# A token-mixing trunk on one core: one head's softmax weights turned by transfers, stores on another queue, turning loads at later steps, last rows in smaller pieces

## The chip, the cores and the metric

The kernel runs on one core of one Trainium2 chip. A core has a matrix engine (TensorE, PE in the profile, with its weight loads as PEld), a vector engine (VectorE, DVE), an activation engine (ScalarE, ACT), GpSimd (POOL), a queue engine (SyncE, SP) and 16 DMA engines that all queues share. SP, ScalarE and GpSimd can issue transfers. The metric is the device time of one execution in microseconds; lower is better.

## The reference

Two layers over 256 latent tokens and 256 context tokens of width 1024, in float32. Layer 0 mixes tokens with a two-way chunked mLSTM of 4 heads, layer 1 with latent attention of 8 heads; each is followed by a gated convolutional FFN, with adaptive modulation and a LayerNorm after every part. The output is the 256 latent rows. The part of the mLSTM that the change touches is, for one head:

```python
dmat = jnp.where(tril, b[..., :, None] - b[..., None, :] + ic[..., None, :], -jnp.inf)
wmat = jnp.exp(dmat - mj[..., None]) * jnp.einsum("bhjd,bhsd->bhjs", qc, kc)
num = g[..., None] * jnp.einsum("bhjd,bhde->bhje", qc, C) + jnp.einsum("bhjs,bhse->bhje", wmat, vc)
h = num / jnp.maximum(jnp.abs(den), jnp.exp(-mj))[..., None]
...
hsum = o * s.transpose(0, 2, 1, 3).astype(h_in.dtype)
return _head_rms_norm(hsum, norm_g) @ w_out
```

and at the very end `(z - mean) * rsqrt(var) * g + b` on the output rows.

## The kernel before

Every float32 product is done as three products of a high and a low part (`mm3`, lines 447, 450, 451): high by high, high by low, low by high. Weights stream from memory through `Stream`: SP loads a block of 128 x 1024 (`raw`), ScalarE casts its high part (line 361), VectorE subtracts the low part (line 384). Three buffers (`NB`) hold split weights, and a buffer is filled again when TensorE is through with it.

The mLSTM is computed without its chunks: for each head `h`, `w_qk(h, ...)` makes queries and keys (four products of 16 blocks, eight weights of 24 matmuls), `s_mm(h)` the scores, `head(h, ...)` the weights of the four row blocks `P[0..3]` (each a tile `W` with an offset), and `av(h)` multiplies them by the values. Row blocks 0 and 1 are context tokens and see only context columns, blocks 2 and 3 see all four column blocks. `av` needs the weights turned, columns on partitions: `head` turns twelve 128 x 128 blocks in three groups of four on TensorE (line 1144) into a PSUM tile `PT`, which `split` cuts into high (ScalarE, line 461) and low part (VectorE, line 462).

`head` is a generator that runs beside the products of the next head. `tick` takes one step of such background work, two steps after each of the eight weights in `w_qk`; `drain` runs what is left. So head 0's weights are made and turned during `w_qk(1)`, and `av(0)` follows it. `post(h, ...)` normalises a head's rows. For heads 0 and 1 it cuts each float32 row into two planes of 16 bits (`planes`, ScalarE, line 466), stores them to DRAM (line 1225, from GpSimd's queue), and `turn_load` (line 1266) loads them transposed from ScalarE's queue; `turn_split` (lines 1274, 1275) scales and cuts them for the output projection. `mixed` interleaves this with the next head's `head` steps by a plan written as a string: each word is a step, `p` a step of `post`, `h` one of `head`, `L` a load, `S` a split.

The program order is a wish: a planner orders each engine's instructions by priority and by its own estimate of when operands are ready, unless an order is pinned. Tiles tagged `s2` (128 x 512 floats, 15 of them) and `u` (31 pairs) are shared by all this work. `ln_rows` with `fin` is the end of the kernel: it normalises two blocks of 128 output rows in halves of 512 columns (lines 1314, 1316; the first half of the first block on ScalarE and GpSimd, lines 1318 to 1320) and stores each half (line 1321), the first half from SP, the second from ScalarE.

Of the kernel before, what the change touches and what calls it, by code (L numbers as in the profile page):

```python
# [10 lines left out]
U16 = mybir.dt.uint16  # L11
AF = mybir.ActivationFunctionType
ALU = mybir.AluOpType
# [21 lines left out]
NB, NRAW, NU, NS = 3, 3, 31, 15  # L35
# [381 lines left out]
class K:  # L417
# [648 lines left out]
    def head(self, h, S, big=False):  # L1066
        nc, last = self.nc, big
        aB = [self.s2("aB0"), self.s2("aB1")]
        for d in range(2):
            nc.gpsimd.dma_start(aB[d], self.ad[d, h:h + 1, :].to_broadcast([128, 512]))  # L1070
        if not big:
            self.t4_step(2)
        Am = [self.s2("Am0"), self.s2("Am1")]
        for d in range(2):
            nc.vector.tensor_tensor(Am[d].rearrange("p (t s) -> p t s", t=4),
                                    aB[d].rearrange("p (t s) -> p t s", t=4),
                                    self.mask[:, d:d + 1, :].to_broadcast([128, 4, 128]), op=ALU.add)
        yield
        full = {0: [(0, 0), (0, 128), (0, 256), (0, 384)], 1: [(128, 256), (0, 0), (0, 256), (0, 256)]}
        P = []  # L1080
        for g in range(3):
            jbs = [0, 1] if g == 0 else [g + 1]
            if big:
                w = self.uf("W")
                W = [w[:, 0:512], w[:, 512:1024]]
            else:
                W = [self.s2("W0"), self.s2("W1")]
            den = self.tiny(4, "den")
            nd = len(jbs)
            rng = {}  # L1090
            for i, t in enumerate(jbs):
                base = 256 * i if g == 0 else 0
                for d in range(2):
                    o = W[d]
                    bias = self.gcol[:, 0, t, 32 * d + h:32 * d + h + 1]
                    spans = [(t * 128, (t + 1) * 128, Am[d])]
                    if d == 0:
                        if t > 0:
                            spans.append((0, t * 128, aB[d]))
                        lo, hi = 0, (t + 1) * 128  # L1100
                    else:
                        if t == 0:
                            spans.append((128, 256, aB[d]))
                        if t >= 2:
                            spans.append((0, 256, aB[d]))
                        if t == 2:
                            spans.append((384, 512, aB[d]))
                        lo, hi = {0: (0, 256), 1: (128, 256), 2: (0, 512), 3: (0, 512)}[t]
                    if d == 1 and t == 3:
                        nc.vector.memset(o[:, 256:384], 0.0)  # L1110
                    for s0, s1, src in spans:
                        nc.scalar.activation(o[:, base + s0:base + s1], src[:, s0:s1], AF.Exp, bias=bias, scale=1.0)
                    nc.vector.scalar_tensor_tensor(o[:, base + lo:base + hi], o[:, base + lo:base + hi], 1.0,
                                                   S[g][:, base + lo:base + hi], op0=ALU.mult, op1=ALU.mult,
                                                   accum_out=den[:, 2 * i + d:2 * i + d + 1])
                    rng[i, d] = (base + lo, base + hi)
            dv = den[:, 0:2 * nd]
            R = self.tiny(4, "R")
            nc.vector.scalar_tensor_tensor(R[:, 0:2 * nd], dv, -1.0, dv, op0=ALU.mult, op1=ALU.max)
            e = self.gcol[:, 1, jbs[0]:jbs[-1] + 1, h::32]  # L1120
            nc.vector.tensor_tensor(R[:, 0:2 * nd].rearrange("p (t d) -> p t d", d=2),
                                    R[:, 0:2 * nd].rearrange("p (t d) -> p t d", d=2), e, op=ALU.max)
            nc.vector.reciprocal(R[:, 0:2 * nd], R[:, 0:2 * nd])
            for i, t in enumerate(jbs):
                big = {0: 1, 1: 0, 2: 1, 3: 0}[t]
                b0, b1 = rng[i, big]
                s0, s1 = rng[i, 1 - big]
                nc.vector.tensor_scalar(W[big][:, b0:b1], W[big][:, b0:b1], R[:, 2 * i + big:2 * i + big + 1], None,
                                        op0=ALU.mult)
                nc.vector.scalar_tensor_tensor(W[big][:, s0:s1], W[1 - big][:, s0:s1],  # L1130
                                               R[:, 2 * i + 1 - big:2 * i + 2 - big], W[big][:, s0:s1],
                                               op0=ALU.mult, op1=ALU.add)
                P.append((W[big], b0))
            yield
        for _ in range(5 if last else 1):
            yield
        self.PT = []
        for grp in ([(t, s) for s in range(2) for t in (0, 1)], [(t, s) for s in range(2) for t in (2, 3)],
                    [(t, s) for s in (2, 3) for t in (2, 3)]):
            pt = self.ps("PT")  # L1140
            lead = None
            for n, (t, s) in sorted(enumerate(grp), key=lambda x: -x[1][0] * (x[1][0] > 1)):
                src, b0 = P[t]
                q = nc.tensor.transpose(pt[:, n * 128:(n + 1) * 128], src[:, b0 + s * 128:b0 + (s + 1) * 128], self.ident)
                if lead is None:
                    lead = q
                elif t > 1:
                    self.behind(q, [lead])
            u = self.u("PT")
            self.split(u[:, 0], u[:, 1], pt)  # L1150
            self.PT.append(u)
        yield

    def v_load(self, h):
# [34 lines left out]
    def av(self, h):  # L1189
        nc = self.nc  # L1190
        PT, v = self.PT, self.vh
        ts = []
        for t in range(4):
            ps = self.ps("av")
            if t < 2:
                blocks = [(PT[0], s, s) for s in range(2)]
            else:
                blocks = [(PT[1], s, s) for s in range(2)] + [(PT[2], s, s + 2) for s in range(2)]
            for n, (u, i, s) in enumerate(blocks):
                c = slice(i * 256 + (t % 2) * 128, i * 256 + (t % 2) * 128 + 128)  # L1200
                self.mm3(ps, (u[:, 0, c], u[:, 1, c]), (v[s][:, 0], v[s][:, 1]), n == 0, n == len(blocks) - 1)
            ts.append(ps)
        for t in range(4):
            nc.vector.tensor_tensor(self.oh[t], ts[t], self.oh[t], op=ALU.mult)
        r = self.oh
        self.PT = self.vh = self.oh = None
        return r

    def post(self, h, tt, last=False):
        nc = self.nc  # L1210
# [9 lines left out]
        if not last:  # L1220
            d = self.dr.tile([512, 2, 512], U16, name="hd")
            for t in range(4):
                pl = self.pool.tile([128, 2, 512], U16, tag="s2", name="pl", bufs=NS)
                self.planes(pl, tt[t])
                nc.gpsimd.dma_start(d[t * 128:(t + 1) * 128], pl)
            self.turned.append((h, d, 0))
            yield
            return
# [15 lines left out]

    def mixed(self, head, post):

        plan = "p hp h hL h hL . L hS LS h S S . . ."
        for step in plan.split():
            for op in step:
                if op in "hp":  # L1250
                    next(head if op == "h" else post, None)
                elif op == "L":
                    self.turn_load()
                elif op == "S":
                    self.turn_split()
            yield
# [29 lines left out]
    def ln_rows(self, pss, xres, gate, fin=None):  # L1286
# [3 lines left out]
        for t in range(2):  # L1290
# [16 lines left out]
            fine = len(pss[1]) > 2  # L1307
            if fin is not None:
                g, b, out = fin
                for c0, c1 in ((0, 512), (512, 1024)):  # L1310
                    c, h = slice(c0, c1), c0 // 512
                    hc = slice(c0 - h * 512, c1 - h * 512)
                    if t or c0 == 512:
                        nc.vector.scalar_tensor_tensor(z[:, c], z[:, c], mv[:, 0:1], g[h][:, hc],
                                                       op0=ALU.subtract, op1=ALU.mult)
                        nc.vector.scalar_tensor_tensor(z[:, c], z[:, c], rs, b[h][:, hc], op0=ALU.mult, op1=ALU.add)
                    else:
                        nc.scalar.activation(z[:, c], z[:, c], AF.Identity, bias=nm, scale=rs)
                        nc.gpsimd.tensor_tensor(z[:, c], z[:, c], g[h][:, hc], op=ALU.mult)
                        nc.gpsimd.tensor_tensor(z[:, c], z[:, c], b[h][:, hc], op=ALU.add)  # L1320
# [1241 lines left out]
```

## Time and profile before

| | |
|---|---|
| median of 3 runs | 1338.72 us (1338.04 to 1338.85) |
| the profiled execution | 1337.94 us |
| its span, first to last instruction | 1336.1 us |
| TensorE busy | 1325.5 us, 99% |
| VectorE, ScalarE, GpSimd busy | 1075.4, 729.0, 165.4 us |
| mean DMA rate | 244 GB/s |
| TensorE in the granted clock | 0.998 |

The span is counted between the first and the last instruction; the execution's own time has 1.84 us around it. In rows of the timeline the columns are start, length, engine, line, operation, output and inputs; in brackets is how long the engine had idled before and whose end released it. Times within the profile are counted from the span's start. ACTq and SPq are the issues of transfers on the queues of these engines.

### The profile page before, as it was taken

What the parts mean: (1) busy time and instruction counts of PE and PEld (TensorE: products, weight loads), DVE (VectorE), ACT (ScalarE), POOL (GpSimd) and SP (SyncE); (2) the same over time, 40 slices, a digit from 0 to 9 for tenths busy, and PEclk for the clock granted to TensorE, in tenths of its full rate; (3) what the DMA queues carried; (4) which work ended last, traced back from release to release, by engine and by line L of the source; (5) the groups of instructions that cost most, each with busy time, mean ns of one, the idle gap of its engine ahead of it and who ended that gap; (6) DMA issues with size and microseconds to landing.
All of it is one profiled execution on the core that took longest, in us unless ns stands there. A gap on an engine that the chain in (4) does not pass through costs nothing.

```text
span 1336.1 us, 18732 instructions
## 1 busy us (share of the span) xinstructions
PE 1325.5 (99%) x6573; PEld 1111.9 (83%) x6573; DVE 1075.4 (80%) x1783; ACT 729.0 (55%) x1271; POOL 165.4 (12%) x268
## 2 busy tenths in 40 slices
PE   9999999999999999999999999999999999999997
PEld 5777888888888888888898888888888988988886
DVE  4798957678688596987879977758899889899995
ACT  4765544445734555574744333333567768577771
POOL 0212000011110111120002011112000022110010
PEclk9999999999999999999999999999999999999999
DMA  9988948789675487876628989967976597499790
GB/s 364 331 276 288 338 160 257 238 270 313 236 262 189 155 248 199 297 275 212 222 79 275 324 259 284 281 174 177 329 232 211 180 244 206 151 309 310 227 334 33
DMA packets 116991, 325.52 MB, mean 244 GB/s; under 512 B 21417, under 2 KB 40361, under 8 KB 116625
## 3 DMA queue, kind: packets, MB, share of 16 engines
q1 hardware_dynamic: 64288, 223.37, 48.9%
q0 software_dynamic: 33360, 81.43, 22.7%
q10 hardware_dynamic: 19248, 19.54, 4.5%
q8 instruction: 51, 0.84, 0.2%
q14 instruction: 44, 0.35, 0.1%
HBM read 289.51 MB, written 56.80 MB: 259 GB/s over the span
## 4 chain that ended last, share of the span: by engine, by line
PE 99%; DMA 0%; DVE 0%; SPq 0%; issue 0%; DVEq 0%; ACT 0%
PE fin L1570 8%; PE y L450 6%; PE y L447 6%; PE y L451 6%; PE tok L447 6%; PE tok L450 6%; PE tok L451 6%; PE fin L450 6%; PE fin L447 6%; PE fin L451 6%; PE qk L447 4%; PE qk L451 4%; PE qk L450 4%; PE up L743 2%; PE up L447 2%; PE up L450 1%
## 5 line engine op out<-in xcount | busy, mean ns | idle before, releaser
L361 ACT CAST w<-raw 128x1024 fp32r<-128x1024 f32 (+2 forms) x280 | 289.8, 1037 | 257.4 <-PE tok L451 73.3
L384 DVE TENSOR_TENSOR w<-raw,w 128x1024 fp32r<-128x1024 f32 (+2 forms) x280 | 335.2, 1200 | 114.7 <-ACT w L361 110.7
L566 DVE SCALAR_TENSOR_TENSOR junk<-ar,bc 128x1024 f32<-128x1024 f32 x128 | 155.7, 1216 | 4.9 <-ACT bc L608 2.6
L450 PE MATMUL fin<-h,w 128*128 128x512 f32 (+1 forms) x370 | 139.6, 377 | 0.0
L447 PE MATMUL fin<-h,w 128*128 128x512 f32 (+1 forms) x370 | 139.5, 377 | 0.0
L451 PE MATMUL fin<-h,w 128*128 128x512 f32 (+1 forms) x370 | 139.3, 377 | 0.0
L1570 PE MATMUL fin<-h,w 128*128 128x512 f32 (+1 forms) x636 | 113.0, 337 | 0.0
L1570 PEld LDWEIGHTS fin<-h,w 128*128 128x128 f32 x636 | 98.4, 189 | 13.4
L447 PE MATMUL qk<-xc,w 128*128 128x512 f32 x256 | 100.1, 391 | 0.0
L451 PE MATMUL qk<-xc,w 128*128 128x512 f32 x256 | 99.7, 389 | 0.0
L450 PE MATMUL qk<-xc,w 128*128 128x512 f32 x256 | 99.6, 389 | 0.0
L447 PEld LDWEIGHTS fin<-h,w 128*128 128x128 f32 x370 | 69.6, 188 | 12.9
L451 PEld LDWEIGHTS fin<-h,w 128*128 128x128 f32 x370 | 69.6, 188 | 12.8
L450 PEld LDWEIGHTS fin<-h,w 128*128 128x128 f32 x370 | 69.6, 188 | 12.7
L384 DVE TENSOR_TENSOR wu<-raw,wu 128x1024 fp32r<-128x1024 f32 (+1 forms) x52 | 61.9, 1206 | 2.8 <-ACT wu L361 2.5
L451 PEld LDWEIGHTS qk<-xc,w 128*128 128x128 f32 x256 | 48.1, 188 | 10.1
L450 PEld LDWEIGHTS qk<-xc,w 128*128 128x128 f32 x256 | 48.1, 188 | 9.9
L447 PEld LDWEIGHTS qk<-xc,w 128*128 128x128 f32 x256 | 48.1, 188 | 9.8
L361 ACT CAST wu<-raw 128x1024 fp32r<-128x1024 f32 (+1 forms) x52 | 52.9, 1046 | 4.9 <-DMA raw<-in_ws 4.9
L760 ACT ACTIVATE fg<-fg 128x512 f32<-128x512 f32 (+1 forms) x44 | 23.1, 525 | 56.3 <-DVE fg L758 50.2
L447 PE MATMUL tok<-w,hT 128*128 128x512 f32 x128 | 49.9, 390 | 0.0
L450 PE MATMUL tok<-w,hT 128*128 128x512 f32 x128 | 49.8, 389 | 0.0
(520 smaller groups left out, 3153.7 us busy)
## 6 DMA issues: line engine op xcount, KB each, us to landing
raw<-in_ws SPq DMA_DIRECT2D x279, 512.0 KB, 5.0
ar<-in_adaT SPq DMA_DIRECT2D x80, 512.0 KB, 5.7
t4d<-in_ws POOLq DMA_DIRECT2D x20, 512.0 KB, 8.2
zd<-in_ws POOLq DMA_DIRECT2D x18, 512.0 KB, 9.9
adaw<-in_ada SPq DMA_DIRECT2D x16, 512.0 KB, 7.9
raw<-zd SPq DMA_DIRECT2D x12, 512.0 KB, 6.1
zr<-fd ACTq DMA_DIRECT2D x33, 128.0 KB, 5.3
xmd<-xr POOLq DMA_DIRECT2D x16, 256.0 KB, 4.7
```

The costliest lines, as they stand in the source:

```text
L361: self.cast = k.nc.scalar.copy(h[:, :cols], src)
L384: i = self.k.nc.vector.tensor_sub(l[:, :n], src, h[:, :n])
L447: q = mm(out, w[0], x[0], start=start, stop=False, skip_group_check=on)
L450: mm(out, w[0], x[1], start=False, stop=False, skip_group_check=on)
L451: mm(out, w[1], x[0], start=False, stop=stop, skip_group_check=on)
L566: nc.vector.scalar_tensor_tensor(o, w, 1.0, self.bc[j], op0=ALU.mult, op1=ALU.mult, accum_out=col[:, k, j:j + 1])
L743: nc.tensor.matmul(ps[m], wk[i][:, c], hT[k][:, j], start=made[m] == 0, stop=made[m] == 23)
L760: nc.scalar.activation(tmp[:, :n], tmp[:, :n], AF.Silu)
L1570: self.nc.tensor.matmul(ps[:, 0:256] if x else ps, w[x][:, k * 128:(k + 1) * 128], h[:, 0:256] if x else h, start=i == 0 and not k0, stop= ...
```

## The change

Head 0's weights are no longer turned on TensorE. `head` hands over to a new generator `head_turn`, which cuts the weights of each row block into 16-bit planes on ScalarE, stores them with six transfers to three DRAM tiles, loads them with six transposing transfers, all from ScalarE's queue, into three `wx` tiles, and splits these into the same high and low parts as before. Its steps fill the sixteen that `w_qk(1)` offers. Heads 1 to 3 turn on TensorE as before. The turned pieces are now kept in a dictionary by (row block, column block), and `av` reads it in the same order.

The plane stores of `post` are issued from ScalarE's queue and not from GpSimd's. The plan of `mixed` has its loads and splits at later steps. In `ln_rows` the second half of the second block of output rows is scaled and stored as two pieces of 256 columns, the first from ScalarE's queue, the second from SP's; the subtraction before it is still one instruction of 512.

```diff
+        if h == 0:
+            yield from self.head_turn(P)
+            return
         for _ in range(5 if last else 1):
             yield
...
+    def head_turn(self, P):
+        nc = self.nc
+        ds = [self.dr.tile([256, 2, 256], U16, name="w%d" % i) for i in range(3)]
+        for g, wait in enumerate((1, 3, 1)):
+            for _ in range(wait):
+                yield
+            pl = self.pool.tile([128, 2, 512], U16, tag="s2", name="pl", bufs=NS)
+            for t, c in ((0, slice(0, 256)), (1, slice(256, 512))) if g == 0 else ((g + 1, slice(0, 512)),):
+                self.planes(pl[:, :, c], P[t][0][:, c])
+            for i in range(2):
+                c = slice(i * 256, (i + 1) * 256)
+                t = i if g == 0 else g - 1
+                nc.scalar.dma_start(ds[1 + i if g else 0][t * 128:(t + 1) * 128], pl[:, :, c])
+        xs = [self.s2("wx") for _ in range(3)]
+        self.PT = {}
+
+        def load(i, j):
+            nc.scalar.dma_start_transpose(xs[i][:, j * 256:(j + 1) * 256].bitcast(U16),
+                                          ds[i].rearrange("t h n -> (t h) n")[:, j * 128:(j + 1) * 128])
+
+        def cut(i):
+            u = self.u("PT")
+            self.split(u[:, 0], u[:, 1], xs[i])
+            for j in range(2):
+                for t in range(2):
+                    self.PT[t + 2 * (i > 0), j + 2 * (i > 1)] = u, slice(j * 256 + t * 128, j * 256 + t * 128 + 128)
+
+        for ls, c in ([(0, 0)], ()), ([(0, 1)], ()), ([(1, 0), (1, 1)], ()), ([(2, 0), (2, 1)], (0,)), ((), (1,)), ((), (2,)):
+            yield
+            for x in ls:
+                load(*x)
+            for x in c:
+                cut(x)
         yield
...
-                nc.gpsimd.dma_start(d[t * 128:(t + 1) * 128], pl)
+                nc.scalar.dma_start(d[t * 128:(t + 1) * 128], pl)
...
-        plan = "p hp h hL h hL . L hS LS h S S . . ."
+        plan = "p hp h h h h . L hL hL L S S S S ."
...
-                for c0, c1 in ((0, 512), (512, 1024)):
+                for c0, c1 in ((0, 512), (512, 768), (768, 1024)) if t else ((0, 512), (512, 1024)):
                     c, h = slice(c0, c1), c0 // 512
                     hc = slice(c0 - h * 512, c1 - h * 512)
                     if t or c0 == 512:
-                        nc.vector.scalar_tensor_tensor(z[:, c], z[:, c], mv[:, 0:1], g[h][:, hc],
-                                                       op0=ALU.subtract, op1=ALU.mult)
+                        if c0 < 768:
+                            x = slice(c0, h * 512 + 512)
+                            nc.vector.scalar_tensor_tensor(z[:, x], z[:, x], mv[:, 0:1], g[h],
+                                                           op0=ALU.subtract, op1=ALU.mult)
                         nc.vector.scalar_tensor_tensor(z[:, c], z[:, c], rs, b[h][:, hc], op0=ALU.mult, op1=ALU.add)
```

More of the change, by code (lines that the diff above doesn't have):

```diff
@@ L1134, in head @@
             yield
+        if h == 0:
+            yield from self.head_turn(P)
+            return
         for _ in range(5 if last else 1):
             yield
-        self.PT = []
+        self.PT = {}
         for grp in ([(t, s) for s in range(2) for t in (0, 1)], [(t, s) for s in range(2) for t in (2, 3)],
@@ L1150, in head @@
             self.split(u[:, 0], u[:, 1], pt)
-            self.PT.append(u)
+            for n, x in enumerate(grp):
+                self.PT[x] = u, slice(n * 128, (n + 1) * 128)
+        yield
[13 more added lines that the diff above has]
+        xs = [self.s2("wx") for _ in range(3)]
+        self.PT = {}
+        def load(i, j):
[8 more added lines that the diff above has]
+        for ls, c in ([(0, 0)], ()), ([(0, 1)], ()), ([(1, 0), (1, 1)], ()), ([(2, 0), (2, 1)], (0,)), ((), (1,)), ((), (2,)):
+            yield
+            for x in ls:
+                load(*x)
+            for x in c:
+                cut(x)
         yield
@@ L1194, in av @@
             ps = self.ps("av")
[L1195 to L1201, printed above, removed]
+            n = 2 if t < 2 else 4
+            for s in range(n):
+                u, c = PT[t, s]
+                self.mm3(ps, (u[:, 0, c], u[:, 1, c]), (v[s][:, 0], v[s][:, 1]), s == 0, s == n - 1)
             ts.append(ps)
```

## The prediction

> **What bounds the kernel now.** I read the page's busy times and its chain first, then the waits of TensorE, then the chain in order of time, then the stages and groups around the edited places.
>
> ```profile
> PE 1325.5 (99%) x6573; PEld 1111.9 (83%) x6573; DVE 1075.4 (80%) x1783; ACT 729.0 (55%) x1271; POOL 165.4 (12%) x268
> PE 99%; DMA 0%; DVE 0%; SPq 0%; issue 0%; DVEq 0%; ACT 0%
> PE idle L680 <- DVE adav L519: 1.5, 1, 1.5
> PE adar L531 <- DMA adaw<-in_ada: 0.3, 1, 0.3
> PE up L743 <- DVE hT L718: 0.3, 1, 0.3
> ```
>
> The last three lines are all the waits TensorE has in the whole span, 2.1 us, and all belong to the start. From there to its last matmul TensorE never waits, and the chain that ended last is 99% TensorE. So two things alone can move the time: the number and pitch of TensorE instructions, and the few microseconds after the last matmul. Work taken off ScalarE, GpSimd or a queue is worth nothing by itself; work put on them costs nothing until it makes TensorE wait. The granted clock is 1.00 in every window row below, so no clock gain is to be had.
>
> **Part 1: head 0's turn leaves TensorE.** The pieces of the chain with the turning instruction of line 1144 (start, length, count), and its group:
>
> ```profile
> 417.25 0.44 PE PT L1144 x4
> 419.76 0.87 PE PT L1144 x8
> 485.36 1.31 PE PT L1144 x12
> L1144 PE MATMUL PT<-ident,W x48: 270/272/275, 417.1 to 590.9; 128*128 128x128 f32 x48
> 400.76:445.60 44.84, 44.84 (x205) 37.25 (x204) 37.03 (x81) 19.49 (x43) 2.68 (x5) 1.00 0.54 173
> ```
>
> 48 instructions in four heads, 12 to a head, each 272 ns long in its row; but they overlap in the pipeline, and on the chain head 0's twelve take 0.44 + 0.87 = 1.31 us, the same as the next head's twelve (1.31). The last line is the stage of head 1's query/key products (window, length, TensorE busy, loads, VectorE, ScalarE, GpSimd, clock, DMA share, GB/s): 44.84 us of 44.84 busy. Without 1.31 it is 43.53 us for its 192 matmuls, 0.227 each. I take 1.31 us off.
>
> What replaces it lies on ScalarE, VectorE and the DMAs. The nearest rows are those of the products that an existing part already turns by transfers (columns min/median/max in ns):
>
> ```profile
> L466 ACT COPY pl<-oh x8: 1038/1046/1054, 458.7 to 519.7; 128x1024 uint16<-128x1024 uint16 x8
> L1266 ACTq DMA_TRANSPOSE hx<-hd x8: 1177/1215/1401, 470.8 to 533.5; - x8
> DMA to landing us min/median/max: 3.2/3.6/4.5
> L848 ACTq DMA_DIRECT2D od<-o x16: 326/327/423, 135.7 to 201.1; - x16
> L1225 POOL DMA_DIRECT2D hd<-pl x8: 539/543/547, 460.0 to 521.1; - x8
> 429.53 1.05 ACT L361 CAST w<-raw 128x1024 fp32r<-128x1024 f32 x1 [3.59 <-PE qk L451]
> 430.62 1.23 DVE L384 TENSOR_TENSOR w<-raw,w 128x1024 fp32r<-128x1024 f32 x1 [1.25 <-ACT w L361]
> ```
>
> ScalarE gets plane copies of 3 x 1024 elements (3 x 1.05 = 3.1 us), six stores (6 x 0.33 = 2.0) and six turning loads (6 x 1.2 = 7.3 if the half-size ones cost as much, 3.6 if they scale). At most 12.4 us, on an engine with 44.84 - 19.49 = 25 us free in that stage. The three casts and three subtractions of the turned weights stay, reading another memory. A load waits on ScalarE's queue for its stores to land, and behind it stand the casts of the next weights (L361), for which TensorE waits. How much it can be held: three weight buffers, each used for 24 x 0.227 = 5.44 us, so a buffer released is needed again 10.9 us later; cast and subtraction were done at 430.62 + 1.23 = 431.85, 2.3 us after the cast's start; 8.6 us are left. A store landing in 3 to 5 us does not use them up. If it did, each further microsecond would be one of TensorE. Cost taken: 0; bounds 0 to the rival's price below. No gain is possible here, as TensorE has no wait to lose.
>
> When the pieces are there: first group of turns starts at 417.09 = 400.76 + 3 x 5.44, exactly after the third weight, where the background's sixth step stands in the code, so TensorE follows the written order. In the new text the last four loads stand after the seventh weight (400.76 + 7 x 5.44 = 438.85). Were they issued only there, the last of them would go at 438.85 + 3 x 1.2 = 442.5, land 3.6 later at 446.1, and be cast and subtracted (0.62 + 0.68) by 447.4.
>
> ```profile
> 445.65 0.39 PE L447 MATMUL av<-v,PT 128*128 128x512 f32 x1
> 418.22 0.75 DVE L1130 SCALAR_TENSOR_TENSOR W<-W,R 128x512 f32<-128x512 f32 x1
> L461 ACT CAST v<-vr x4: 619/622/622, 435.5 to 437.0; 128x512 fp32r<-128x512 f32 x4
> L462 DVE TENSOR_TENSOR v<-vr,v x4: 684/684/685, 436.2 to 438.0; 128x512 fp32r<-128x512 f32 x4
> 457.99 0.39 PE L447 MATMUL qk<-xc,w 128*128 128x512 f32 x1
> 475.79 1.26 ACTq L1266 DMA_TRANSPOSE hx<-hd  x1
> ```
>
> The product with the values would start at 445.65 - 1.31 = 444.3, and it reaches the third piece after 18 matmuls, at 444.3 + 4.1 = 448.4: 1.0 us spare in the latest order. In the earliest order (weights of the last row block ready at 418.97, copy, store and load after it, some 10 us) the pieces are there by 430. The planner issues such loads ahead of their place in the text: head 2's products start at 457.99, the fourth turning load stands there after the fifth weight (457.99 + 27.2 = 485.2), and it went at 475.79. So I take the early case: no wait.
>
> **Part 2: plane stores from GpSimd's queue to ScalarE's, later turning loads.** Eight stores leave GpSimd (8 x 0.54 = 4.3 us) for ScalarE (8 x 0.33 = 2.6 us, two stages). On GpSimd they stood waiting for the copies, with the broadcasts of the next head's gates behind them:
>
> ```profile
> POOL hd L1225 <- ACT pl L466: 82.3, 6, 49.2
> DVE Am L1075 <- DMA aB<-ad: 15.1, 4, 5.9
> 470.71 0.40 ACT L1112 ACTIVATE W<-Am,gcol 128x128 f32<-128x128 f32 x1 [4.09 <-DVE Am L1075]
> 445.00:491.00 46.00, 46.00 (x216) 38.47 (x215) 31.55 (x70) 28.23 (x57) 8.54 (x16) 1.00 0.75 224
> 475.00:480.00 5.00, 5.00 (x24) 4.14 (x23) 4.93 (x16) 3.15 (x10) 2.96 (x6) 1.00 1.05 173
> 485.00:490.00 5.00, 5.00 (x30) 4.27 (x29) 4.87 (x8) 3.95 (x7) 0.54 (x1) 1.00 1.04 401
> raw<-in_ws SPq DMA_DIRECT2D x1, 512.0 KB, 8.3
> raw<-in_ws SPq DMA_DIRECT2D x279, 512.0 KB, 5.0
> 486.05 1.05 ACT L361 CAST w<-raw 128x1024 fp32r<-128x1024 f32 x1 [4.24 <-DMA raw<-in_ws]
> ```
>
> Those broadcasts can go earlier, and ScalarE's 4.09 us at 470.71 shrink. TensorE is busy 46.00 of 46.00 us in that stage regardless, so this is worth 0 between the bounds: no gain, and no loss while ScalarE has 18 us idle. The turning loads are hard on the DMAs: all engines taken at 173 GB/s where plain transfers reach 401 at the same share, and one weight load beside them landed after 8.3 us against 5.0; a cast waited 4.24 us for it, and even so TensorE did not. Loads placed later meet the value loads instead; the cover is again the three buffers. The splits of the turned rows move a few steps later inside the same stage, and their first reader is the output projection after the next stages. Cost 0.
>
> The Trainium skill, "Advanced Engine Details and Errata", section X-Bar Transpose (TRN2), holds transposing DMAs to be as fast as regular ones, about 90% of a copy. The two 5 us windows (173 against 401 GB/s) disagree, and the measurement decides. By the page, contention in either stage would be no rival; the sum is the same by both.
>
> **Part 3: last rows in smaller transfers.** What follows the last matmul:
>
> ```profile
> 1328.16 0.42 DVE L1297 SCALAR_TENSOR_TENSOR z<-xres,z 128x256 f32<-128x256 f32 x1
> 1330.89 0.66 DVE z L1316
> 1330.81 1.41 DVE L1316 SCALAR_TENSOR_TENSOR z<-z,rs,br 128x512 f32<-128x512 f32 x2
> 1332.25 0.34 ACTq L1321 DMA_DIRECT2D out_dram<-z  x1
> DMA to landing us min/median/max: 2.1/2.1/2.1
> GB/s 0 0 0 0 0 0 0 82 377 385 205 0 0 0 0 0 0 0 0 0 0 82 393 360 377 393 369 99 33 25 0 0 0 0 0 0 0 0 0 0
> ```
>
> The second half of the second row block is now scaled and shifted as two pieces of 256 columns instead of one of 512. One of 512 takes 0.66 us in the chain, one of 256 between 0.33 and 0.44 (the dependent 0.42 plus its gap): the last piece is ready 0 to 0.22 us later; I take 0.08. Its transfer is half as large: the present one lands 2.1 us after issue, and its 0.26 MB at some 380 GB/s are 0.69 us, so half saves 0 to 0.34. But the first half's transfer still starts at the same time and the rate row (0.23 us a slice) shows the engines full from there on, so little of it comes through; I take 0.18. Together -0.1, bounds -0.34 to +0.22.
>
> **Sum.** -1.31 - 0.1 = -1.41 us. The profiled execution took 1337.94 us (span 1336.1 and 1.84 around it), so it would be 1336.5; the median of the runs shown is 1338.72, 0.78 above the profiled one, and on it the forecast is 1337.3 us, -0.11%. About 0.2% (2.7 us) is what a measurement of this kernel can tell from no change, so this counts as within it.
>
> **The rivals.**
> *Late turned weights (slower).* The last turning load meets other transfers on full DMA engines and takes as long as such transfers took beside the other turning loads:
>
> ```profile
> oh<-od POOLq DMA_DIRECT2D x2, 256.0 KB, 10.3
> ```
>
> 10.3 instead of 3.6 in the latest order makes the third piece late by 6.7 - 1.0 = 5.7 us; TensorE waits in the product with the values: 1337.3 + 5.7 = 1343.0 us. It is slower by over 0.2% from 4.1 us of wait on, a landing 8.7 us after issue in that order. For it: the 8.3 and 10.3 us rows. Against it: this stage has a DMA share of 0.54, and the early order has 15 us more. Chance 0.12.
>
> *A small wait somewhere (no measurable change).* All engines' orders after the edit are planned anew, and a wait of 1 to 4 us where there is none now, in this stage or a later one, eats the gain or turns it: 1338.3 to 1341.3, 1339.8 in the middle. For it: margins like the 1.0 us above, and the cast that waited 4.24. Against it: 2.1 us of waits in the whole span. Chance 0.22.
>
> *Each turn is worth its whole row (faster).* If the twelve cost their 272 ns and not their chain share, 12 x 0.272 = 3.3 us go: 1338.72 - 3.3 - 0.1 = 1335.3, -0.25%. Against it: the stage's 44.84 us hold 192 matmuls of 0.227 and leave 1.31. Chance 0.06.
>
> *Fewer small transfers win at the end.* If the last transfer's landing does not shrink with its size and the extra instruction costs its 0.22, part 3 is +0.22: 1337.6. The Trainium skill, "SBUF — State Buffer", section The DMA setup-cost knee, speaks for it: about 2 us a transfer whatever its size, so coalesce. Its fit gives an estimate of 2.6 us for 256 KB and 2.3 for 128 KB; the row has 2.1 for 256 KB, below both. It changes the hundredths only and lies inside the main case.
>
> **How the numbers follow.** Main case 0.60 at 1337.3, its own range 1336.7 to 1338.0; the small wait 0.22, late weights 0.12, the whole row 0.06. Within 0.2%: 0.60 + 0.22 = 0.82; slower 0.12; faster 0.06. The range takes the main case, nearly all of the small wait and the lower half way to 1335.3: 1336.2 to 1340.8.
>
> **What will show it.** Twelve instructions of line 1144 fewer, and TensorE idle still only in the start's waits: right. The stage of head 1's products at 43.5 us: right. A wait of the value product on the turned weights, or of any matmul on a weight's subtraction: wrong, by its length. The last output transfer issued near 1331.0 (1332.25 - 1.31 + 0.08) and the span ending 3.7 us after it (now 3.85) would confirm the tail. A cast held over 8 us behind a turning load would refute the cover I named.

## The result: slower, and the profile after

| | before | after |
|---|---|---|
| median, measured together | 1338.38 us (1337.82 to 1338.85, 4 runs) | 1357.07 us (1351.47 to 1360.96, 4 runs) |
| the profiled execution | 1337.94 us | 1358.53 us |
| its span | 1336.1 us | 1356.6 us |

The ratio is 1.0135, 95% interval 1.0115 to 1.0154. The forecast was 1337.3 us, its upper bound 1340.8. The four executions after the change lie 9.5 us apart; what follows is read from one of them.

The page's busy times and clock digits of the changed kernel (40 slices of 33.9 us), then every wait of TensorE (total us, times, longest):

```profile
PE 1330.7 (98%) x6561; PEld 1115.2 (82%) x6561; DVE 1074.9 (79%) x1784; ACT 731.6 (54%) x1275; POOL 161.2 (12%) x260
PEclk9999999999999979999999999999999999999999
PE PT L1147 <- DVE W L1130: 15.8, 3, 10.8
PE idle L680 <- DVE adav L519: 1.5, 1, 1.5
PE up L743 <- DVE hT L718: 0.3, 1, 0.3
```

Twelve instructions fewer on TensorE, as the change says, yet 5.2 us more busy time, and a wait that did not exist: TensorE's turn of the weights of heads 1 to 3 (`PT`, now line 1147) waits for VectorE's last scaling of `W` in all three heads, 10.8, 0.9 and 4.1 us. The longest begins near 484.65, in the middle of head 2's query and key products, where head 1's weights are turned. What ScalarE, VectorE and GpSimd did there (start, length; in brackets the idle time before and what ended it; ACTq is the issue of a transfer on ScalarE's queue):

```profile
468.27 1.26 ACTq L1304 DMA_TRANSPOSE hx<-hd  x1
473.37 1.18 ACTq L1304 DMA_TRANSPOSE hx<-hd  x1
474.58 7.19 ACTq L1304 DMA_TRANSPOSE hx<-hd  x1
481.86 11.34 ACTq L1304 DMA_TRANSPOSE hx<-hd  x1
493.24 0.19 ACT L581 COPY adav<-w 1x1 f32<-1x1 f32 x1 [11.14 <-issue]
493.34 0.57 ACT L461 CAST qk<-qk 128x512 fp32r<-128x512 f32 x1
493.94 0.69 DVE L462 TENSOR_TENSOR qk<-qk 128x512 fp32r<-128x512 f32 x1 [10.27 <-ACT qk L461]
494.55 0.74 DVE L1130 SCALAR_TENSOR_TENSOR W<-W,R 128x512 f32<-128x512 f32 x1
495.44 1.94 PE L1147 MATMUL PT<-ident,W 128*128 128x128 f32 x8 [10.79 <-DVE W L1130]
471.86 2.18 POOL L1200 DMA_DIRECT2D vr<-vd  x4 [26.11 <-DVE W L1113]
474.14 0.63 POOL L1206 DMA_DIRECT2D oh<-od  x1
```

Read it upwards from TensorE's row. The turn waited for the scaling of `W`, which took only 0.74 us, but stood on VectorE behind the subtraction of `qk`; that waited 10.27 us for ScalarE's cast; and the cast stood on ScalarE's queue behind the *issues* of the third and fourth turning loads, which held the engine for 7.19 and 11.34 us. The product that it casts was done by about 479 (the products start at 456.85, and its four weights take 4 x 5.44 us); in the kernel before, the same cast ran at 479.95. Before the change an issue took at most 1.40 us. Nothing in the data orders the scaling of `W` behind a turning load: two in-order queues did.

What the long issues have beside them is seen in the neighbours: GpSimd's loads of the values and gates (`vr`, `oh`) start at 471.86, and three of the four turning loads after them. In the kernel before, the four went at 470.83 to 475.79, the first value load at 475.70. The turning loads' group and landing before, the same after, and the DMA queues in a window of before (470.5 to 475) and two of after (480 to 490, 490 to 500), as packets, MB and share of the 16 engines; q10 holds the turning loads, q0 GpSimd's:

```profile
L1304 ACTq DMA_TRANSPOSE hx<-hd x8: 1176/2504/11335, 468.3 to 549.5; - x8
DMA to landing us min/median/max: 18.8/19.3/20.9
...
q10 hardware_dynamic: 2010, 0.51, 68.8%
...
q10 hardware_dynamic: 1260, 0.31, 61.2%
q0 software_dynamic: 212, 0.68, 48.0%
...
q10 hardware_dynamic: 1646, 0.41, 68.9%
```

(The 3.2/3.6/4.5 us landing of before stands in the prediction.) Before, turning loads moved 0.51 MB in 4.5 us, some 113 GB/s, with a quarter of the engines' time going to SP's plain loads. After, they moved 0.31 MB in 10 us beside the value and gate loads and 0.41 MB in the next 10 us, in which SP's plain loads (34.8%) had mostly taken the place of these: 31 and 41 GB/s, though the turning loads take about as large a share of the engines. Landing went from 3.6 to 19.3 us.

The windows across the wait (window, length; busy us of TensorE, its loads, VectorE, ScalarE, GpSimd; granted clock, DMA share, GB/s):

```profile
484.00:486.00 2.00, 0.65 (x5) 0.36 (x3) 0.00 (x0) 0.00 (x0) 0.54 (x1) 1.00 1.51 100
486.00:488.00 2.00, 0.00 (x0) 0.00 (x0) 0.00 (x0) 0.00 (x0) 0.00 (x0) 0.92 1.10 102
488.00:490.00 2.00, 0.00 (x0) 0.00 (x0) 0.00 (x0) 0.00 (x0) 0.00 (x0) 0.50 1.38 77
498.00:500.00 2.00, 2.00 (x6) 1.58 (x5) 1.91 (x3) 0.70 (x3) 0.00 (x0) 0.50 1.01 353
502.00:503.00 1.00, 1.00 (x6) 0.81 (x5) 1.00 (x1) 0.00 (x0) 0.00 (x0) 1.00 0.22 86
608.00:610.00 2.00, 1.94 (x9) 1.98 (x10) 1.92 (x5) 0.59 (x1) 0.00 (x0) 0.50 0.80 260
612.00:614.00 2.00, 2.00 (x6) 1.58 (x5) 0.92 (x3) 0.00 (x0) 0.00 (x0) 0.50 1.03 412
614.00:616.00 2.00, 2.00 (x14) 1.72 (x13) 0.00 (x0) 0.19 (x1) 0.00 (x0) 1.00 0.40 158
```

All compute engines stand still between 486 and 490 while the DMA engines are full at 77 to 102 GB/s. The clock falls to half some 3 us into the wait, and stays there for 6 us of work after it (495.44 to about 501.4): that work takes about 3 us more than at full clock. The same follows the 4.1 us wait (608.06 to 614). So: 15.8 us of waits, two times about 3 us at half clock, less 1.3 us for the twelve turns, make about 20.5, as much as the span's 1356.6 - 1336.1.

The 4.1 us wait, in head 3, is not a hold by a turning load: the last of these issues ended at 549.47 + 4.76 = 554.23, some 50 us earlier. There ScalarE's casts had waited for weights to land, 4.57, 5.52, 1.51 and 4.01 us between 567 and 589, and the last two ran 21 us later than before, in a kernel then 13 us behind (waits of 10.8 and 0.9, 3 at half clock, less 1.3; first line before, second after):

```profile
568.04 2.00 ACT L361 CAST wu<-raw 128x1024 fp32r<-128x1024 f32 x2 [1.43 <-DMA raw<-in_ws]
589.20 2.00 ACT L361 CAST wu<-raw 128x1024 fp32r<-128x1024 f32 x2 [4.01 <-DMA raw<-in_ws]
```

VectorE was then busy almost without a gap until `W` was scaled. So some 7 of the 20 us (the wait and its half clock) most likely come of weights that were late, not of the engine that was held. The turning loads that landed up to about 570 are a likely cause, as the runs below without the meeting have no wait there; no run separates the two parts.

### The profile page after: what moved, and what is told of

Same layout as the page of the kernel before. It is cut to its first block, busy times and chain, and to the rows that moved or that the text cites. A ratio compares the mean times of both kernels' runs of the same rounds, so it can differ in the third digit from the quotient of the medians.

```text
span 1356.6 us, 18741 instructions
## 1 busy us (share of the span) xinstructions
PE 1330.7 (98%) x6561; PEld 1115.2 (82%) x6561; DVE 1074.9 (79%) x1784; ACT 731.6 (54%) x1275; POOL 161.2 (12%) x260
## 4 chain that ended last, share of the span: by engine, by line
PE 54%; DVE 2%; DMA 1%; issue 1%; ACT 0%; DVEq 0%
PE fin L1610 8%; PE fin L450 6%; PE fin L451 6%; PE fin L447 6%; PE y L450 6%; PE y L447 6%; PE y L451 6%; PE y L1453 1%; PE fin L1546 1%; PE s L2338 1%; DMA raw<-in_ws 1%; PE PT L2359 1%; DMA ar<-in_adaT 0%; PE zT L1401 0%; DVE w L384 0%
## 5 line engine op out<-in xcount | busy, mean ns | idle before, releaser
L447 PEld LDWEIGHTS qk<-xc,w 128*128 128x128 f32 x256 | 48.6, 190 | 10.2
L450 PEld LDWEIGHTS qk<-xc,w 128*128 128x128 f32 x256 | 48.6, 190 | 10.1
L451 PEld LDWEIGHTS qk<-xc,w 128*128 128x128 f32 x256 | 48.5, 189 | 10.2
```

Of the source, the lines that this page charges most:

```text
L447: q = mm(out, w[0], x[0], start=start, stop=False, skip_group_check=on)
L450: mm(out, w[0], x[1], start=False, stop=False, skip_group_check=on)
L451: mm(out, w[1], x[0], start=False, stop=stop, skip_group_check=on)
```

## The experiments

Medians beside the kernel before on the same chip (pooled 1338.4 us). First the change was taken apart.

**The new plan alone**, in the kernel before:

```diff
-        plan = "p hp h hL h hL . L hS LS h S S . . ."
+        plan = "p hp h h h h . L hL hL L S S S S ."
```

> The kernel before with nothing changed but the plan of the mixed steps (turning loads and splits later). Theory A (the later turning loads run into the value loads, are starved, and their issue holds ScalarE): slower than before by 8 to 25 us, the turning instruction of heads 1 and 2 waiting on VectorE for W, issues of the third and fourth turning load over 3 us. Theory B (the stores on ScalarE's queue are what holds it) and theory C (head 0's six stores and six loads are what holds it): within 0.2% of before, no TensorE wait after the start.

Measured 1359.42 us, ratio 1.0168 (1.015 to 1.0186): the whole loss, as theory A had it (only the third issue stayed under its 3 us). ScalarE's turning loads and TensorE's wait:

```profile
475.87 1.31 ACTq L1266 DMA_TRANSPOSE hx<-hd  x1
477.21 2.62 ACTq L1266 DMA_TRANSPOSE hx<-hd  x1
479.97 12.64 ACTq L1266 DMA_TRANSPOSE hx<-hd  x1
PE PT L1144 <- DVE W L1130: 16.9, 2, 9.1
```

The loads go only some 4 us later than before (474.56 for the first, against 470.83), the value loads at 475.75 as ever. That is enough: the fourth issue holds ScalarE 12.64 us. In the next head it does so for 11.57 us, and both of TensorE's waits here (9.1 and 7.8 us) come behind such an issue.

**The new stores alone**, in the kernel before:

```diff
-                nc.gpsimd.dma_start(d[t * 128:(t + 1) * 128], pl)
+                nc.scalar.dma_start(d[t * 128:(t + 1) * 128], pl)
```

> The kernel before with nothing changed but the eight plane stores, issued from ScalarE's queue. Theory A: within 0.2% of before (1338), no TensorE wait after the start, turning loads issued in 1.2 to 1.5 us each. Theory B: slower by 8 to 25 us. Theory C: within 0.2%.

Measured 1339.32 us, ratio 1.0022 (1.0003 to 1.0041), at most a small loss in the median, which refutes theory B (8 to 25 us). But theory A's issues of 1.2 to 1.5 us did not hold either: the longest is 5.92 us. The stores let GpSimd send the value loads earlier, which brings the two kinds closer together from the other side. TensorE has no new wait in the profile, though only just:

```profile
476.83 5.92 ACTq L1266 DMA_TRANSPOSE hx<-hd  x1
485.17 0.74 DVE L1130 SCALAR_TENSOR_TENSOR W<-W,R 128x512 f32<-128x512 f32 x1
485.44 1.68 PE L1144 MATMUL PT<-ident,W 128*128 128x128 f32 x12
```

The last scaling of `W` ends 0.5 us after the turn that reads it has begun, and the twelve turns take 1.68 us where they took 1.47. The ten executions run from 1337.66 to 1350.71 us, the profiled one took 1338.63: in some the slack was likely not enough, but none of those has a profile.

**Everything but the plan**: the changed kernel with the first of these edits; **everything but plan and stores**: with both.

```diff
-        plan = "p hp h h h h . L hL hL L S S S S ."
+        plan = "p hp h hL h hL . L hS LS h S S . . ."
...
-                nc.scalar.dma_start(d[t * 128:(t + 1) * 128], pl)
+                nc.gpsimd.dma_start(d[t * 128:(t + 1) * 128], pl)
```

> The changed kernel with the old plan of the mixed steps. Theory A: 1.3 to 1.5 us under before (ratio 0.9985 to 0.9995), no TensorE wait after the start. Theory B and theory C: slower than before by 8 to 25 us.

> The changed kernel with the old plan and the old stores, so only head 0's turn by transfers and the smaller last transfers. Theory A and theory B: 1.3 to 1.5 us under before (1337). Theory C: slower by 8 to 25 us.

The first measured 1338.13 us (1336.43 to 1343.28), ratio 1.0006 (0.9995 to 1.0018), with 1.5 us of wait on `W` in head 3 and a longest issue of 4.21 us; theory A had expected 1.3 to 1.5 us less than before and no wait, so it held in the main only, while B and C, 8 us or more slower, are refuted. The second measured 1336.82 us, 0.9991 (0.9981 to 1.0), about as A and B expected, with no wait but the start's and issues of 1.91 us at most. The turning loads of the first landed after a median of 18.9 us, as late as in the changed kernel, and its median is only 1.3 us over the second's: nearly all of a late landing is covered. What differs most from the changed kernel is how long ScalarE is held.

Then the cause: the meeting of two kinds of loads, or the plan's order itself?

**No value loads.** The changed kernel without the transfers that the turning loads meet:

```diff
-            nc.gpsimd.dma_start(r, self.vd[h, s])
+            if h == 0:
+                nc.gpsimd.dma_start(r, self.vd[h, s])
+            else:
+                nc.gpsimd.memset(r, 0.5)
```

and the same for the gates `oh`. GpSimd fills the tiles with a constant, so what heads 1 and 2 should compute is left out.

> The changed kernel without the sixteen value and gate loads of heads 1 and 2: GpSimd fills their tiles with a constant instead, so what those heads compute is left out; ScalarE's order is the same as in the changed kernel. Theory A (the value loads beside them starve the turning loads): turning loads issue in under 2.5 us each and land in under 8, no wait of the turning instruction on W, and the time is 1335 to 1339. Rival (the later place, four loads close together, is enough): issues of 5 to 12 us remain and the time stays at 1350 to 1360.

Measured 1336.84 us, 0.9989 (0.998 to 0.9998), as theory A had it. The same plan, the same queue, and the issues of the turning loads are short again:

```profile
L1310 ACTq DMA_TRANSPOSE hx<-hd x8: 1176/1262/1802, 467.4 to 532.8; - x8
DMA to landing us min/median/max: 5.1/5.4/6.3
```

So the new order of the engines' work costs nothing by itself; it needs the other transfers beside it.

**The new plan with turning loads on SP's queue**, in the kernel before (the plan's line as above):

```diff
-        self.nc.scalar.dma_start_transpose(x.bitcast(U16), d.rearrange("t h n -> (t h) n")[:, e * 128:(e + 1) * 128])
+        self.nc.sync.dma_start_transpose(x.bitcast(U16), d.rearrange("t h n -> (t h) n")[:, e * 128:(e + 1) * 128])
```

> The kernel before with the new plan, and the turning loads issued from SP's queue instead of ScalarE's; the same transfers meet on the DMA engines. If the cost is ScalarE standing in the issue (theory A's second half): the turning instruction's waits of 17 us go, ScalarE shows no idle time ahead of a gate copy put down to issue, and the time is under 1346; the issues of 5 to 12 us are then SP's. Rival (the data on the crowded DMA engines is late whichever queue issues them, weights and values above all): 1350 to 1362, with TensorE waiting for weights instead.

Measured 1338.0 us, 0.9998 (0.9989 to 1.0008). No loss, but the experiment did not tell what it was made for: SP was free earlier and sent the loads ahead of the value loads (474.98), so both the meeting and ScalarE's hold were gone. The issues expected at 5 to 12 us on SP took 4.12 at most.

```profile
467.08 8.51 SPq L1266 DMA_TRANSPOSE hx<-hd  x4
```

**The same, held back to meet the value loads.** Each head's turning loads are tied behind an earlier weight load on SP:

```diff
+        if e == 0:
+            self.anchor = self.st.sent[-3]
+        with self.tc.issue_after(self.anchor.ins):
+            self.nc.sync.dma_start_transpose(...)
```

(The plan's line and the list `st.sent` of the weight loads are left out here.)

> The kernel before with the new plan alone, but the turning loads of heads 1 and 2 go out from SP's queue instead of ScalarE's, and are tied to an earlier raw load so that they start at about 477 us, beside the value and gate loads vr and oh, as in the changed kernel. Theory (ScalarE held while it issues): the loads should still land late (over 10 us) and an issue on SP's queue may take 5 to 12 us, but ScalarE's casts of qk are not held, so the wait of TensorE's turn PT for W is under 3 us; time 1337 to 1343 us, unless the weights wx themselves come late. Rival (the crowded transfers make data late whichever queue issues them): TensorE waits 8 us or more for wx, W or the values, and the time is 1350 us or more.

Measured 1352.91 us, 1.0101 (1.0083 to 1.012). Neither expectation held whole: the time is the rival's, but no single wait of 8 us is there. SP's queue, then VectorE, then TensorE:

```profile
477.78 13.61 SPq L1269 DMA_TRANSPOSE hx<-hd  x3
485.14 1.47 PE L1144 MATMUL PT<-ident,W 128*128 128x128 f32 x12
503.99 1.23 DVE L566 SCALAR_TENSOR_TENSOR junk<-ar,bc 128x1024 f32<-128x1024 f32 x1 [7.70 <-DMA ar<-in_adaT]
506.57 0.50 PE L450 MATMUL av<-v,PT 128*128 128x512 f32 x1 [3.37 <-DVE v L462]
PE PT L1144 <- DVE W L1130: 3.4, 1, 3.4
PE qk L447 <- ACT w L361: 1.4, 1, 1.4
PE qk L451 <- DVE w L384: 1.1, 1, 1.1
```

With ScalarE free, head 1's turn at 485.14 did not wait at all: the 9.1 us at this place with the new plan alone, and by the same chain the 10.8 us of the changed kernel, are indeed ScalarE's hold. But now SP was held (13.61 us for three issues, 15.41 in the next head), and behind these stood the loads of weights and of `ar`; VectorE waited 7.70 us for `ar` with the subtraction of the values behind it, and TensorE for that; further waits followed near 544 and 602. TensorE's idle time in the span rose from 1336.1 - 1325.5 = 10.6 to 1350.6 - 1331.6 = 19.0 us, its busy time by 6.1. The collision costs on either queue; which queue issues the loads decides who is late.

**The changed kernel with all turning loads on SP**, head 0's and the others', not held back:

```diff
-            nc.scalar.dma_start_transpose(xs[i][:, j * 256:(j + 1) * 256].bitcast(U16),
+            nc.sync.dma_start_transpose(xs[i][:, j * 256:(j + 1) * 256].bitcast(U16),
...
-        self.nc.scalar.dma_start_transpose(x.bitcast(U16), d.rearrange("t h n -> (t h) n")[:, e * 128:(e + 1) * 128])
+        self.nc.sync.dma_start_transpose(x.bitcast(U16), d.rearrange("t h n -> (t h) n")[:, e * 128:(e + 1) * 128])
```

> The changed kernel with one edit: every turning load goes out from SP's queue, none from ScalarE's; stores stay on ScalarE's queue. Theory (ScalarE held in the issue is the loss): the loss goes, 1336.5 to 1339 us, PT's wait for W under 2 us, although SP may send the loads earlier than ScalarE did. Rival (the new plan's order of the engines' work costs time by itself, or the loads come late from any queue): 1345 us or more.

Measured 1336.94 us, 0.999 (0.998 to 0.9999), as the theory had it. All 20 us are back, with the changed kernel's plan and stores:

```profile
L1304 SPq DMA_TRANSPOSE hx<-hd x8: 1166/1263/1849, 465.9 to 527.8; - x8
DMA to landing us min/median/max: 6.9/6.9/6.9
```

SP sends them from 465.88, ahead of the values, and each issue is short. This says that sending them early is enough, not that SP is the better queue.

**What the rest is worth.** Head 0's turn alone in the kernel before, and turn with the last rows' pieces (the changed kernel with old plan and old stores, run again):

```diff
+        if h == 0:
+            yield from self.head_turn(P)
+            return
```

> The kernel before with head 0's turn by transfers and nothing else. If the end of the kernel gains 0.2 us by the smaller transfers, this is 0.2 us over the run with turn and rows together, 1.3 to 1.4 us under before: ratio 0.9990. If the smaller transfers cost there, it is under that run.

> The version with head 0's turn and the smaller last transfers once more, in five rounds: 1.4 to 1.6 us under before, ratio 0.9988 to 0.9990, and the interval does not reach 1.

1337.32 us, 0.9992 (0.9983 to 1.0001), and 1337.36 us, 0.999 (0.9981 to 0.9999). The second came 1.1 us under before, a little less than the 1.4 to 1.6 expected. The pieces' own share is not resolved by these. Turn and rows without plan and stores, the turn alone, and the changed kernel with its loads on SP are level, about 0.1% faster than the kernel before; no form that was run is better.

The longest issue of a turning load, and what it did:

| kernel | queue | longest issue, us | median landing, us | new waits of TensorE | median, us |
|---|---|---|---|---|---|
| before | ScalarE | 1.40 | 3.6 | none | 1338.4 |
| turn and rows | ScalarE | 1.91 | 4.4 | none (0.5 when run again) | 1336.8 |
| new stores alone | ScalarE | 5.92 | 6.7 | none | 1339.3 |
| all but the plan | ScalarE | 4.21 | 18.9 | 1.5, in head 3 | 1338.1 |
| changed | ScalarE | 11.34 | 19.3 | 15.8, of it 4.1 in head 3 | 1357.1 |
| new plan alone | ScalarE | 12.64 | 19.0 | 16.9 | 1359.4 |
| no value loads | ScalarE | 1.80 | 5.4 | none | 1336.8 |
| new plan, loads on SP | SP | 4.12 | 5.1 | 0.2 | 1338.0 |
| new plan, SP, held back | SP | 7.61 | 16.6 | 9.3 | 1352.9 |
| changed, all loads on SP | SP | 1.85 | 6.9 | none | 1336.9 |

A hold of 6 us left no wait on TensorE in the profiled execution (and at most 0.4% in the median), but used up the slack there; issues of 11 to 13 us cost waits of 8 to 11. So the cover on ScalarE ends near 6 us. It is not one number for every place: in the changed kernel's next head, issues of 3.50 and 4.76 us in a row cost 0.9 us. The waits in head 3 come some 50 us after the last long issue and are not explained by it.

## Why the prediction was wrong, point by point

**Part 2 failed, at one step: "Loads placed later meet the value loads instead; the cover is again the three buffers. [...] Cost 0".** It saw the meeting, and the two rows that make it costly stood beside it: 173 GB/s on full engines, and a weight load beside turning loads landing after 8.3 us and not 5.0. Two things were missed. First, it priced the meeting as a late landing of something, when the item that cost most is the issue: 1.2 us became 11.34, nearly all of it time in which ScalarE runs nothing. The rows of before had issues of 1.18 to 1.40 us only, since few plain transfers came beside the loads there; that is no bound for the case in which more do. Second, it asked only what the three weight buffers cover. The instruction that was late was none of the weights': it was the cast of `qk`, and through VectorE's order the scaling of `W`, for which TensorE's turn in the middle of the products waits with no buffer between. The question that part 1 asked of head 0's loads would have led there: what is queued behind the waiting instruction on ScalarE, and then who waits for that on VectorE. The part's bound "no loss while ScalarE has 18 us idle" took a mean over the stage for slack at a place.

**The test named for it came out against it.** "A cast held over 8 us behind a turning load would refute the cover": the cast at 493.34 stands behind 11.14 us in which ScalarE ran nothing, some 14 us after its product was done.

**Part 1 was right in size.** From the first matmul of head 1's query products to that of head 2's there were 457.99 - 400.76 = 57.23 us before, and in the turn-and-rows kernel:

```profile
400.60 0.39 PE L447 MATMUL qk<-xc,w 128*128 128x512 f32 x1
456.46 0.39 PE L447 MATMUL qk<-xc,w 128*128 128x512 f32 x1
400.76:444.20 43.44, 43.44 (x194) 35.97 (x193) 35.65 (x80) 22.73 (x47) 4.31 (x8) 1.00 0.85 227
```

55.86 us, 1.37 less against 1.31 forecast, and TensorE busy throughout. In the changed kernel too the turned pieces were in time, but later than the early case had them (ready by 430). Their loads landed after 7.0 us and not 3.6, and the last subtraction ended at 443.2 + 0.68 = 443.9, for a product that starts at 444.51 and needs the third piece 4.1 us later:

```profile
L462 DVE TENSOR_TENSOR PT<-wx,PT x3: 679/680/680, 442.0 to 443.2; 128x512 fp32r<-128x512 f32 x3
DMA to landing us min/median/max: 7.0/7.0/7.0
444.51 0.39 PE L447 MATMUL av<-v,PT 128*128 128x512 f32 x1
```

The stage's DMA share rose from the 0.54 of before to the 0.85 of the window above, which the step did not count.

**Part 3 is not shown.** In the turn-and-rows kernel the last matmul ends at 1325.88 + 0.28 and the span at 1334.4, 8.24 us later; before, 8.44. That is -0.2 against -0.1, inside the bounds of -0.34 to +0.22. But the same stretch took 7.8 to 8.75 us in the six profiles with the old last rows (8.28 with the turn alone) and 8.0 to 8.25 in the six with the new ones, so neither sign nor size can be told. The last output transfer goes at 1330.9, as named (1331.0), and the span ends 3.5 us after it (3.7 named).

**The sum** of parts 1 and 3 alone, 1337.3 us, is what the turn-and-rows kernel measured: 1336.82 and 1337.36.

**The rivals.** *Late turned weights* (0.12) had the right kind of cause, transfers in each other's way, at the wrong loads and with the wrong price: head 0's were in time, and of the old ones of the turned rows it was the issue that cost. *A small wait* (0.22) was what happened without the new plan (0.5 to 1.5 us on `W`), which the turn's gain outweighs or evens out; with the plan the waits came to 15.8 us, outside its 1 to 4. Nothing in the rivals counted the clock, which added about 6 us to the waits: the row of 1.00 in every window was taken as the absence of a gain, not as something to lose.

**Transposing loads.** The Trainium skill, "Advanced Engine Details and Errata", section X-Bar Transpose (TRN2), holds transposing transfers to be about as fast as regular ones. The measurement decided against it in the prediction, and it does so more strongly here: 31 to 41 GB/s beside value and weight loads. Having said so, the prediction then used the disagreement for nothing.

**On the clock**, the waits do not set a fixed price. Two windows of the run with the loads held back on SP, the first after its 3.4 us wait for the values (503.2 to 506.57), the second after its 3.4 us wait for `W` (601.85 to 605.25):

```profile
508.00:510.00 2.00, 2.00 (x7) 1.52 (x5) 2.00 (x3) 1.32 (x3) 0.00 (x0) 0.50 0.72 268
606.00:608.00 2.00, 2.00 (x11) 1.66 (x10) 2.00 (x4) 1.00 (x2) 0.54 (x1) 1.00 0.98 307
```

The first cost 3.4 us at half clock, the second none. With the new plan alone, 3.0 and 4.6 us of work ran at half clock after waits of 9.1 and 7.8 us, against 5.9 after both waits in the changed kernel. All stretches at half clock in the profiles of the three slower kernels (idle time included) last 3.4, 6.8, 10.2 or 13.7 us, multiples of 3.4. The Trainium skill, "TensorE: Matmul & The Clock Gate", section What's actually happening, says that the array's clock falls to half after an idle window of about 3.4 us and comes back after one of sustained work, and that this window is free-running. The trace agrees: the stretches are whole numbers of such windows, and where a wait falls among them decides how much work is slow.

## What to carry to other kernels

Moving transfers to a later step is a change of what they run beside: list, from the timeline, what the DMA engines do at the new place, and price the issue as well as the landing, on the queue of the issuing engine. Then follow each in-order queue behind the issuing engine until it reaches the bound engine; slack counted over a stage is no slack at a place. Where the bound engine idles for some 3 us or more, half clock can follow: here 3 to 6 us of work after such waits, once none.

## What the runs showed of the hardware that was not expected

- The issue of a transposing load can hold the issuing engine: 1.2 to 1.9 us each for the loads of the rows on ScalarE where it was short, up to 12.64 us for one (new plan alone) beside plain transfers of 256 KB, and 15.41 us for three on SP. On ScalarE the long ones were the third and fourth of a group. Why the issue is held, no run shows.
- Transposing loads lose far more beside plain ones than these do: 113 GB/s to 31 to 41, median landing 3.6 to 19.3 us, while the median landing of `oh` went from 6.1 to 10.1.
- TensorE's half clock after a wait comes in stretches of 3.4, 6.8, 10.2 or 13.7 us here, and waits of 3.4 us were followed by one such stretch and by none.
